# Value projection of the scans: four jobs of three token tiles by 256 channels become three jobs of two tiles by 512

## Chip, core and metric

One core of one Trainium2 chip. The time is the device time of one execution, in microseconds (us). The core's engines run their own instruction queues in order and meet on semaphores: TensorE (PE, matmuls; its weight loads are PEld), VectorE (DVE), ScalarE (ACT), GpSimd (POOL), and SyncE (SP), which issues the loads from HBM.

## The reference, cut to what matters

Two layers of a hybrid token mixer over 512 latent and 256 context tokens (768 rows here, D = 1024), all in fp32. Each layer projects the normed tokens `h` by one wide matrix and cuts the columns among three branches:

```
z = h @ w_in                       # (768, 1024) @ (1024, D_IN)
(aq, ak, av, gq, gk, gv, gr, ga, rq, rk, rv, rg, mg) = split_in(z)
o_a = window_attention(qa, ka, va, ...)              # 8 heads of 64, 2 key heads
o_g = bidir_scan(gq, gk, gv, decays from ga)         # gated linear attention, 4 heads, dv 128
o_r = bidir_scan(rq, rk, rv, fixed decays)           # retention, 4 heads, dv 128
y = sum(sigmoid(mg_z) * (o_z @ w_branch_z)) @ w_out  # merge, then a gated MLP with a convolution
```

The change concerns the two value projections `gv` and `rv` of each layer: 768 tokens by 1024 rows by 512 channels, four times in the program (two scans, two layers). Their results are wanted with tokens on the partitions.

## The kernel before

The program is one list of jobs, walked by `flow` (L486). An ordinary job (`chunk`, L457) makes 128 output channels for all tokens: the weight block is stationary, the tokens `h` stream by in pieces of 512 and 256 columns. Precision is kept by splitting weights and tokens into a high and a low part: three passes per 128-row block k, high by high, high by low, low by high. Tokens come split in `hh` and `hl`. Weights are split job by job in `split_w` (L431): a raw tile of 128x512 is loaded by SP (`load`, L421), ACT copies it to the high part (L452), and DVE or POOL subtracts (L454) to give the low one. All three tiles come from one ring of 12 buffers (`wp`, L319).

A value job (`Wide`, L208, `chunk_wide` L474) turns the roles round: a 128-token tile of `h` is stationary and the weights stream by, so that the result has tokens on the partitions. `value_jobs` (L915) makes four jobs per scan: two halves of 256 channels, each by tiles 0 to 2 and 3 to 5. A raw tile holds two row blocks of 256 channels, so a half takes four loads and four splits; the second job of a half shares the first one's (`share`). The gated linear attention's splits are subtracted on POOL (`job.pool`), the retention's on DVE. In `flow` (L531 to L547) a value job with its own weights finds the first two splits made during the job before and puts the other two into the queues after its first row block; a shared one puts those of the next job there. `prev.evac` (after the first row block of the next job) moves the finished PSUM tile to SBUF on ACT.

Beside the jobs runs side work, written as generators that put a step into the queues at every `yield`: `att_mix` (L816, window attention) beside the jobs of gated linear attention, `gla_mix` (L981) beside those of retention. Each pass of a job calls `beat` (L374), which adds the pass's matmul budget times a rate (`RATE`, L188: 2.0 and 1.65 steps per us beside gated linear attention, 0.693 and 0.655 beside retention, in layers 0 and 1) and issues a step for each whole unit. The budget of a scan's value jobs is 31.1 us (`cost`, L216), before and after the change; that of an ordinary job is 7.8 us (5.2 with 512 tokens). So the order on every engine is the program's order: a split stands behind each side step issued before it. `gla_mix` is hooked to the second value job of the retention (`J[1].pre`, L1357); it has 36 steps in layer 0 and 30 in layer 1, and is drained at the first gate job (`beside`, L1331). Its first phase runs three functions staggered over the six tiles: `logits` (one matmul L998, ACT L1000 to L1002, DVE L1003, ACT L1005, POOL L1006), `decays` (L1008) and `states` (L1084).

Of the kernel before, what the change touches and what calls it, by code (L numbers as in the profile page):

```python
# [11 lines left out]
AF = mybir.ActivationFunctionType  # L12
# [5 lines left out]
L, D, KD = 2, 1024, 8  # L18
TL, TC = 512, 256
TA = TL + TC  # L20
# [64 lines left out]
def pack(a):  # L85

    A = {k: np.asarray(v) for k, v in a.items()}
    f = np.float32

    def kp(m):  # L90
        return m.reshape(-1, 128, m.shape[-1]).transpose(1, 0, 2)

    def units(w):
        K, N = w.shape
        return w.reshape(K // 128, 128, N // 128, 128).transpose(2, 1, 0, 3)

    def wide(w):
        K, N = w.shape
        return w.reshape(K // 128, 128, N // 256, 256).transpose(2, 1, 0, 3)

    def rows(v, n=128):
        return np.broadcast_to(v, (n,) + v.shape).reshape(n, -1)

    r = {}
    r["x0"] = kp(np.concatenate([A["x"][0].T, A["ctx"][0].T], 1))
    con, ret = constants()
    r["con"], r["rcon"] = con, ret
    s = {}
    s["cc"] = kp(np.stack([A["c"][0], A["c_ctx"]], 1)).reshape(128, 16)
    s["adab"] = A["ada_b"].reshape(2, 48, 128).transpose(2, 0, 1).reshape(128, 96)  # L110
    s["n1g"] = A["norm1_g"].reshape(2, 8, 128).transpose(2, 0, 1).reshape(128, 16)
    s["n2g"] = A["norm2_g"].reshape(2, 8, 128).transpose(2, 0, 1).reshape(128, 16)
    s["qg"] = np.tile(A["attn_q_norm_g"].T, (2, 1))
    s["kg"] = np.tile(A["attn_k_norm_g"].T, (2, 1))
    s["sink"] = rows(A["attn_sink"])
    s["gng"] = A["gla_out_norm_g"].T
    s["rng"] = A["ret_out_norm_g"].T
    rd = A["ret_log_decay"]
    s["reta"] = rows(rd)
    pr = rd.reshape(2, 2, 2, 2)  # L120
    s["retb"] = np.concatenate([rows(pr[..., 0], 64), rows(pr[..., 1], 64)], 0)
    s["retc"] = np.concatenate([rows(rd[:, 0], 64), rows(rd[:, 1], 64)], 0)
    s["cw"] = A["ffn_conv_w"].reshape(2, 3, 44, 128).transpose(3, 0, 2, 1).reshape(128, 264)
    s["cb"] = A["ffn_conv_b"].reshape(2, 44, 128).transpose(2, 0, 1).reshape(128, 88)
    r["sml"] = np.concatenate([s[k] for k in SML], 1)

    r["ada"] = A["ada_w"][0][:, :2048].reshape(2, 4, 128, 2, 8, 128)[:, :, :, ::-1].transpose(4, 0, 2, 1, 3, 5)
    adt = A["ada_w"].transpose(0, 2, 1).reshape(2, 48, 128, 2, 512)
    r["adv"] = adt.transpose(0, 3, 1, 2, 4)
    r["crow"] = rows(np.stack([A["c"][0], A["c_ctx"]]).reshape(2, 2, 512).transpose(1, 0, 2))  # L130
    wi = A["w_in"]
    v0 = 512 + 128 + 128 + 256 + 256
    g0 = v0 + 512 + 512
    v1 = g0 + 32 + 256 + 256
    main = np.concatenate([wi[:, :, :v0], wi[:, :, v0 + 512:g0], wi[:, :, g0 + 32:v1], wi[:, :, v1 + 512:]], 2)
    r["wv"] = np.stack([np.stack([wide(wi[l, :, v:v + 512]) for v in (v0, v1)]) for l in range(L)])
    r["win"] = np.stack([units(main[l]) for l in range(L)])
    r["wga"] = np.stack([kp(wi[l, :, g0:g0 + 32]) for l in range(L)])
    gw = np.zeros((2, 98, 512), f)
    for n in (0, 32, 64):  # L140
        gw[:, n:n + 16, 0:256] = A["gla_gate_w"][:, 0]
        gw[:, n + 16:n + 32, 256:512] = A["gla_gate_w"][:, 1]
    gw[:, 96:98] = A["gla_gate_b"].reshape(2, 1, 512)
    r["gw"] = gw
    wb = A["w_branch"].copy()

    wb[:, 0] = wb[:, 0].reshape(2, 2, 4, 64, D).transpose(0, 2, 1, 3, 4).reshape(2, 512, D)
    r["wbr"] = np.stack([np.stack([units(wb[l, z]) for z in range(3)]) for l in range(L)])
    r["wo"] = np.stack([units(A["w_out"][l]) for l in range(L)])
    r["up"] = np.stack([units(A["ffn_up"][l]) for l in range(L)])  # L150
    r["dn"] = np.stack([units(A["ffn_down"][l]) for l in range(L)])
    return {k: np.ascontiguousarray(v.reshape(shape(k))) for k, v in r.items()}
# [1 line left out]

SHAPES = {
    "x0": (128, KD * TA), "con": (128, NCON), "rcon": (128, 512), "sml": (128, NSML),
    "ada": (16, 128, 1024), "adv": (L, 2, 48, 128, 512), "crow": (128, 2048), "win": (L, 46, 128, 1024), "wv": (L, 2, 2, 128, 2048), "wga": (L, 128, 256), "gw": (L, 98, 512),
    "wbr": (L, 3, 8, 128, 512), "wo": (L, 8, 128, 1024), "up": (L, 44, 128, 1024),
    "dn": (L, 8, 128, NFF * 128),
}  # L160
# [33 lines left out]
class Job:  # L194


    def __init__(self, src, h, cols, evac, nk=8, m=128, pre=None, share=None, late=False):
        self.src, self.h, self.cols, self.evac = src, h, cols, evac
        self.nk, self.m, self.pre, self.share, self.late = nk, m, pre, share, late
        self.ps = None  # L200
        self.raw, self.w, self.home, self.eager = [], [], None, ()
        self.pool = self.early = False
        self.wide, self.kp = False, 4

        self.both = m <= 64


class Wide(Job):  # L208


    def __init__(self, src, h, t0, evac, share=None):
        Job.__init__(self, src, h, [(0, TA)], evac, m=256, share=share)
        self.t0, self.wide, self.kp = t0, True, 2


def cost(cols):  # L216
# [96 lines left out]
class Prog:  # L313
# [117 lines left out]
    def split_w(self, job, part=1):  # L431

        if job is None:
            return
        if job.share:
            job.w = job.share.w
            return
        nc = self.nc
        self.load(job)
        for raw, n in job.raw[len(job.w):part + 1]:  # L440
            by_k = lambda v: v[:, 0:n].rearrange("p (k c) -> p k c", c=job.m)
            if job.home:
                k = job.kp * len(job.w)
                hi, lo = (v[:, k:k + n // job.m] for v in job.home())
            elif job.both:
                m = job.m
                both = self.wp.tile([128, 512], F32R, name="wb", tag="w")[:, 0:2 * n].rearrange("p (k c) -> p k c", c=2 * m)
                hi, lo = both[:, :, 0:m], both[:, :, m:2 * m]
            else:
                hi, lo = (by_k(self.wp.tile([128, 512], F32R, name=f"w{p}", tag="w")) for p in "hl")  # L450
            raw = by_k(raw)
            nc.scalar.activation(out=hi, in_=raw, func=AF.Copy)  # L452
            eng = nc.gpsimd if job.pool else nc.vector
            eng.tensor_tensor(out=lo, in0=raw, in1=hi.bitcast(F32), op=ALU.subtract)  # L454
            job.w.append((hi, both) if job.both else (hi, lo))

# [17 lines left out]
    def chunk_wide(self, job, k):  # L474

        nc = self.nc
        if job.ps is None:
            job.ps = self.pg()
        for n, (a, b) in enumerate(((0, 0), (1, 0), (0, 1))):
            for t in range(3):  # L480
                o = 128 * (job.t0 + t)
                nc.tensor.matmul(job.ps[:, 256 * t:256 * t + 256], job.h(k, b)[:, o:o + 128], job.w[k // 2][a][:, k % 2, :],  # L482
                                 start=(k == 0 and n == 0 and t != 1), stop=(k == job.nk - 1 and n == 2 and t > 0))
            self.beat(cost(job.cols) / 3)

    def flow(self, jobs):  # L486
# [5 lines left out]
        for item in jobs:  # L492
# [36 lines left out]
            self.split_w(job)  # L529
            n1, n2 = nxt(job, 1), nxt(job, 2)  # L530
            if job.wide:  # L531
                n3 = nxt(job, 3)
                for k in range(job.nk):
                    self.chunk_wide(job, k)
                    if k == 0:
                        prev.evac(prev.ps)
                    if not job.share:
                        if k == 0:
                            self.split_w(job, 3)
                        if k == 2:  # L540
                            self.load(n2, 4)
                            if not n2.wide:
                                self.load(n3)
                    elif k % 2 and (n1.wide or k == 3):
                        self.split_w(n1, k // 2)
                prev = job
                continue  # L547
            for k in range(job.nk):
# [366 lines left out]
    def value_jobs(self, l, scan, v):  # L915

        nc = self.nc

        jobs = []
        for j in range(2):  # L920
            for t in (0, 3):
                def evac(ps, j=j, t=t):
                    nc.scalar.activation(out=v()[:, t:t + 3, 256 * j:256 * j + 256],
                                         in_=ps[:, 0:TA].rearrange("p (t c) -> p t c", c=256), func=AF.Copy)

                jobs.append(Wide(self.i["wv"][l, scan, j], self.h, t, evac, jobs[-1] if t else None))
        return jobs


    def gla_jobs(self, l, nq):  # L930
# [775 lines left out]
```

## Time and profile before

| | |
|---|---|
| median of 3 runs | 2346.07 us (2345.8 to 2353.48) |
| profiled execution | 2355.63 us, span 2353.8 us |
| granted TensorE clock | 0.998 of full speed |
| PE busy | 2305.4 us, 98% |
| DVE / ACT / POOL busy | 60% / 40% / 13% |
| value matmuls (L482) | 1152 of 128x256, in four stretches from 151.5 to 1623.9 us |

In the profile's lines, L482 is the matmul of the value jobs, L470 that of the ordinary ones; `pg` is a job's PSUM tile, `wh` and `wl` are the weights' high and low parts, `raw` the loaded tile. "x3" counts merged instructions, an arrow reads "output from inputs", and brackets hold the idle time before an instruction with what ended it. PE's matmuls overlap, so the distance between starts, not the duration, is what one costs.

### The profile page before, as it was taken

Reading aid. Unit: us, or ns where it says so; the run is one execution under the profiler, and the core shown is the slowest. Engines: PE = TensorE matmul, PEld = TensorE weight load, DVE = VectorE, ACT = ScalarE, POOL = GpSimd, SP = SyncE. Lnnn points to the kernel's source line nnn. Section 1 sums busy time; section 2 is a strip of 40 time slices with the busy share of each in tenths; the row PEclk is TensorE's granted clock in tenths of the full one; section 3 lists DMA queues with packets and bytes.
Section 4 is the critical chain, followed back from the end, with each engine's and each line's share of the span. In section 5 each row is a group of like instructions: output and inputs, shape, how many; then the busy total and the mean of one; then the engine's idle time right before and its main releaser. Section 6 shows DMA issues by size and latency. Waiting matters only on the chain.

```text
span 2353.8 us, 35262 instructions
## 1 busy us (share of the span) xinstructions
PE 2305.4 (98%) x13570; PEld 1982.2 (84%) x13570; DVE 1415.1 (60%) x2870; ACT 930.5 (40%) x1622; POOL 298.8 (13%) x256
## 2 busy tenths in 40 slices
PE   7999999999999999999999999999999999999999
PEld 4888888888888888888888887989888888888887
DVE  5665475523777578766686656546753555645564
ACT  4665633322323253313313347555443335434342
POOL 0111164000111020000000014113500111000000
PEclk9999999999999999999999999999999999999999
DMA  7111112322454333353253331111333333232333
GB/s 257 54 39 46 44 59 90 95 65 79 139 161 157 104 95 118 120 186 97 88 188 99 96 106 65 50 46 38 101 114 112 95 103 113 97 96 98 99 99 99
DMA packets 132840, 235.79 MB, mean 100 GB/s; under 512 B 14460, under 2 KB 25980, under 8 KB 132544
## 3 DMA queue, kind: packets, MB, share of 16 engines
q1 hardware_dynamic: 123200, 223.57, 29.6%
q10 hardware_dynamic: 9472, 9.96, 1.2%
q8 instruction: 107, 1.75, 0.3%
q14 instruction: 61, 0.50, 0.1%
HBM read 220.37 MB, written 13.11 MB: 99 GB/s over the span
## 4 chain that ended last, share of the span: by engine, by line
PE 87%; DVE 5%; ACT 3%; issue 2%; POOL 1%; DMA 1%; SPq 0%; POOLq 0%; ACTq 0%; DVEq 0%
PE pg L470 73%; PE pg L482 5%; PE pm L908 2%; PE pm L897 1%; PE pm L1089 1%; PE ps L845 1%; PE ps L844 1%; PE pm L1111 1%; DVE qs L1052 1%; PE pm L1112 1%; DVE P L890 0%; PE pm L1275 0%; PE pm L613 0%; DVE Sg L1102 0%; DMA og<-o 0%
## 5 line engine op out<-in xcount | busy, mean ns | idle before, releaser
L470 PE MATMUL pg<-hh,wh 128*128 128x512 f32 (+1 forms) x2384 | 726.1, 357 | 6.6 <-DVE X L1317 1.5
L470 PE MATMUL pg<-hh,wl 128*128 128x512 f32 (+1 forms) x2384 | 722.2, 355 | 0.3 <-POOL wl L454 0.3
L470 PE MATMUL pg<-hl,wh 128*128 128x512 f32 (+1 forms) x2384 | 720.4, 354 | 0.9 <-POOL hl L305 0.7
L454 DVE TENSOR_TENSOR wl<-raw,wh 128x512 fp32r<-128x512 f32 x500 | 356.9, 722 | 335.8 <-ACT wh L452 284.0
L470 PEld LDWEIGHTS pg<-hh,wh 128*128 128x128 f32 x2384 | 397.5, 189 | 74.7 <-issue 4.5
L452 ACT ACTIVATE wh<-raw 128x512 fp32r<-128x512 f32 (+1 forms) x556 | 334.2, 619 | 309.6 <-PE pg L470 123.1
L470 PEld LDWEIGHTS pg<-hl,wh 128*128 128x128 f32 x2384 | 397.2, 189 | 66.3 <-POOL hl L305 1.4
L470 PEld LDWEIGHTS pg<-hh,wl 128*128 128x128 f32 x2384 | 395.4, 189 | 62.7 <-issue 1.3
L652 DVE SCALAR_TENSOR_TENSOR junk<-adr,crow 128x512 f32<-128x512 f32 x256 | 193.6, 756 | 9.1 <-DMA adr<-adv 2.9
L454 POOL TENSOR_TENSOR wl<-raw,wh 128x512 fp32r<-128x512 f32 x56 | 75.7, 1366 | 763.5 <-PE pg L470 556.4
L470 PE MATMUL pg<-al,wh 128*128 128x512 f32 (+1 forms) x500 | 154.2, 356 | 1.4 <-DVE al L572 1.4
L470 PE MATMUL pg<-ah,wh 128*128 128x512 f32 (+1 forms) x500 | 155.0, 358 | 0.0
L470 PE MATMUL pg<-ah,wl 128*128 128x512 f32 (+1 forms) x500 | 154.7, 357 | 0.0
L1306 POOL TENSOR_TENSOR M<-M,sg 128x768 f32<-128x768 f32 (+1 forms) x30 | 58.3, 1942 | 538.2 <-DVE sg L1304 538.2
L1294 ACT ACTIVATE sg<-pg 128x768 f32<-128x768 f32 (+1 forms) x48 | 33.7, 702 | 215.4 <-PE pg L470 215.4
L1479 DVE SCALAR_TENSOR_TENSOR acc<-pg,sml,acc 128x511 f32<-128x511 f32 (+1 forms) x129 | 84.8, 658 | 38.5 <-ACT acc L1476 38.3
L1317 DVE SCALAR_TENSOR_TENSOR X<-pg,mod,X 128x512 f32<-128x512 f32 (+1 forms) x72 | 45.7, 659 | 90.7 <-PE pg L470 90.7
L1476 ACT ACTIVATE acc<-pg,sml 128x768 f32<-128x768 f32 (+1 forms) x86 | 75.5, 878 | 59.6 <-PE pg L470 59.5
L470 PEld LDWEIGHTS pg<-al,wh 128*128 128x128 f32 x500 | 83.7, 188 | 16.9 <-DVE al L572 2.3
L470 PEld LDWEIGHTS pg<-ah,wh 128*128 128x128 f32 x500 | 83.9, 188 | 14.7 <-ACT ah L571 0.4
L470 PEld LDWEIGHTS pg<-ah,wl 128*128 128x128 f32 x500 | 83.4, 188 | 13.9
L1481 DVE SCALAR_TENSOR_TENSOR acc<-pg,sml,acc 128x511 f32<-128x511 f32 (+1 forms) x129 | 85.3, 661 | 4.6
(280 smaller groups left out, 3027.6 us busy)
## 6 DMA issues: line engine op xcount, KB each, us to landing
raw<-win SPq DMA_DIRECT2D x184, 256.0 KB, 2.9
raw<-up SPq DMA_DIRECT2D x176, 256.0 KB, 2.9
adr<-adv SPq DMA_DIRECT2D x160, 256.0 KB, 3.1
raw<-dn SPq DMA_DIRECT2D x64, 256.0 KB, 2.9
raw<-wbr SPq DMA_DIRECT2D x48, 256.0 KB, 2.7
aw<-ada SPq DMA_DIRECT2D x32, 256.0 KB, 5.4
raw<-wv SPq DMA_DIRECT2D x32, 256.0 KB, 3.1
raw<-wo SPq DMA_DIRECT2D x32, 256.0 KB, 3.0
```

The source lines that it names most:

```text
L452: nc.scalar.activation(out=hi, in_=raw, func=AF.Copy)
L454: eng.tensor_tensor(out=lo, in0=raw, in1=hi.bitcast(F32), op=ALU.subtract)
L470: nc.tensor.matmul(job.ps[0:m, lo:hi], job.w[k // 4][a][:, k % 4, :], job.h(k, b)[:, lo:hi], start=(k == 0 and n == 0), stop=(k == job.nk ...
L482: nc.tensor.matmul(job.ps[:, 256 * t:256 * t + 256], job.h(k, b)[:, o:o + 128], job.w[k // 2][a][:, k % 2, :], start=(k == 0 and n == 0 an ...
L652: nc.vector.scalar_tensor_tensor(out=junk, in0=raw, scalar=1.0, in1=cr[v], op0=ALU.mult, op1=ALU.mult, accum_out=acc)
L908: nc.tensor.matmul(po[64 * kv:64 * kv + 64, 0:256], self.att["Va"][:, kb, 64 * kv:64 * kv + 64], PT[b][:, 256 * kv:256 * kv + 256], start= ...
L1294: nc.scalar.activation(out=sgs[d][:, 0:n], in_=ps[:, 0:n], func=AF.Tanh, scale=0.5)
L1306: eng.tensor_tensor(out=m, in0=m, in1=sg[:, 0:n], op=ALU.add)
L1317: nc.vector.scalar_tensor_tensor(out=X(d)[:, lo:hi], in0=ps[:, lo:hi], scalar=gate(d, int(lo >= TL)), in1=xin[:, lo:hi], op0=ALU.mult, op1 ...
L1476: nc.scalar.activation(out=acc[:, 0:nq], in_=ps[:, 0:nq], func=AF.Identity, scale=cw(1), bias=self.s("cb", 44 * l + u))
L1479: nc.vector.scalar_tensor_tensor(out=acc[:, lo + 1:hi], in0=ps[:, lo:hi - 1], scalar=cw(0), in1=acc[:, lo + 1:hi], op0=ALU.mult, op1=ALU.add)
L1481: nc.vector.scalar_tensor_tensor(out=acc[:, lo:hi - 1], in0=ps[:, lo + 1:hi], scalar=cw(2), in1=acc[:, lo:hi - 1], op0=ALU.mult, op1=ALU.add)
```

## The change

Each scan's values become three jobs of two token tiles by all 512 channels, with 512-column matmuls. A job no longer shares weights: each of the three loads all eight row blocks (128x512, one per raw tile) and splits them. The loads go out five row blocks ahead, the splits two, spread over the job; from the last blocks on they are those of the next job. The subtract alternates between DVE and POOL. A job fills a PSUM tile of 1024 columns, evacuated in one piece, and the weights are packed to match.

```diff
--- before.py
+++ after.py
@@ -94,10 +94,6 @@
         K, N = w.shape
         return w.reshape(K // 128, 128, N // 128, 128).transpose(2, 1, 0, 3)
 
-    def wide(w):
-        K, N = w.shape
-        return w.reshape(K // 128, 128, N // 256, 256).transpose(2, 1, 0, 3)
-
     def rows(v, n=128):
         return np.broadcast_to(v, (n,) + v.shape).reshape(n, -1)
 
@@ -133,7 +129,7 @@
     g0 = v0 + 512 + 512
     v1 = g0 + 32 + 256 + 256
     main = np.concatenate([wi[:, :, :v0], wi[:, :, v0 + 512:g0], wi[:, :, g0 + 32:v1], wi[:, :, v1 + 512:]], 2)
-    r["wv"] = np.stack([np.stack([wide(wi[l, :, v:v + 512]) for v in (v0, v1)]) for l in range(L)])
+    r["wv"] = np.stack([np.stack([kp(wi[l, :, v:v + 512]) for v in (v0, v1)]) for l in range(L)])
     r["win"] = np.stack([units(main[l]) for l in range(L)])
     r["wga"] = np.stack([kp(wi[l, :, g0:g0 + 32]) for l in range(L)])
     gw = np.zeros((2, 98, 512), f)
@@ -154,7 +150,7 @@
 
 SHAPES = {
     "x0": (128, KD * TA), "con": (128, NCON), "rcon": (128, 512), "sml": (128, NSML),
-    "ada": (16, 128, 1024), "adv": (L, 2, 48, 128, 512), "crow": (128, 2048), "win": (L, 46, 128, 1024), "wv": (L, 2, 2, 128, 2048), "wga": (L, 128, 256), "gw": (L, 98, 512),
+    "ada": (16, 128, 1024), "adv": (L, 2, 48, 128, 512), "crow": (128, 2048), "win": (L, 46, 128, 1024), "wv": (L, 2, 128, 4096), "wga": (L, 128, 256), "gw": (L, 98, 512),
     "wbr": (L, 3, 8, 128, 512), "wo": (L, 8, 128, 1024), "up": (L, 44, 128, 1024),
     "dn": (L, 8, 128, NFF * 128),
 }
@@ -208,9 +204,9 @@
 class Wide(Job):
 
 
-    def __init__(self, src, h, t0, evac, share=None):
-        Job.__init__(self, src, h, [(0, TA)], evac, m=256, share=share)
-        self.t0, self.wide, self.kp = t0, True, 2
+    def __init__(self, src, h, t0, evac):
+        Job.__init__(self, src, h, [(0, 1024)], evac, m=512)
+        self.t0, self.wide, self.kp = t0, True, 1
 
 
 def cost(cols):
@@ -450,7 +446,7 @@
                 hi, lo = (by_k(self.wp.tile([128, 512], F32R, name=f"w{p}", tag="w")) for p in "hl")
             raw = by_k(raw)
             nc.scalar.activation(out=hi, in_=raw, func=AF.Copy)
-            eng = nc.gpsimd if job.pool else nc.vector
+            eng = nc.gpsimd if (len(job.w) % 2 if job.wide else job.pool) else nc.vector
             eng.tensor_tensor(out=lo, in0=raw, in1=hi.bitcast(F32), op=ALU.subtract)
             job.w.append((hi, both) if job.both else (hi, lo))
 
@@ -476,11 +472,12 @@
         nc = self.nc
         if job.ps is None:
             job.ps = self.pg()
-        for n, (a, b) in enumerate(((0, 0), (1, 0), (0, 1))):
-            for t in range(3):
+        hi, lo = job.w[k]
+        for n, (w, b) in enumerate(((hi, 0), (lo, 0), (hi, 1))):
+            for t in range(2):
                 o = 128 * (job.t0 + t)
-                nc.tensor.matmul(job.ps[:, 256 * t:256 * t + 256], job.h(k, b)[:, o:o + 128], job.w[k // 2][a][:, k % 2, :],
-                                 start=(k == 0 and n == 0 and t != 1), stop=(k == job.nk - 1 and n == 2 and t > 0))
+                nc.tensor.matmul(job.ps[:, 512 * t:512 * t + 512], job.h(k, b)[:, o:o + 128], w[:, 0, :],
+                                 start=(k == 0 and n == 0), stop=(k == job.nk - 1 and n == 2))
             self.beat(cost(job.cols) / 3)
 
     def flow(self, jobs):
@@ -529,20 +526,21 @@
             self.split_w(job)
             n1, n2 = nxt(job, 1), nxt(job, 2)
             if job.wide:
-                n3 = nxt(job, 3)
+
                 for k in range(job.nk):
                     self.chunk_wide(job, k)
                     if k == 0:
                         prev.evac(prev.ps)
-                    if not job.share:
-                        if k == 0:
-                            self.split_w(job, 3)
-                        if k == 2:
-                            self.load(n2, 4)
-                            if not n2.wide:
-                                self.load(n3)
-                    elif k % 2 and (n1.wide or k == 3):
-                        self.split_w(n1, k // 2)
+                    if k < 4:
+                        self.load(job, k + 5)
+                    elif n1.wide:
+                        self.load(n1, k - 3)
+                    elif k % 2 == 0:
+                        self.load(n1 if k == 4 else n2)
+                    if k < 6:
+                        self.split_w(job, k + 2)
+                    else:
+                        self.split_w(n1, k - 6)
                 prev = job
                 continue
             for k in range(job.nk):
@@ -916,15 +914,10 @@
 
         nc = self.nc
 
-        jobs = []
-        for j in range(2):
-            for t in (0, 3):
-                def evac(ps, j=j, t=t):
-                    nc.scalar.activation(out=v()[:, t:t + 3, 256 * j:256 * j + 256],
-                                         in_=ps[:, 0:TA].rearrange("p (t c) -> p t c", c=256), func=AF.Copy)
-
-                jobs.append(Wide(self.i["wv"][l, scan, j], self.h, t, evac, jobs[-1] if t else None))
-        return jobs
+        def evac(t):
+            return lambda ps: nc.scalar.activation(out=v()[:, t:t + 2, :], in_=ps.rearrange("p (t c) -> p t c", c=512), func=AF.Copy)
+
+        return [Wide(self.i["wv"][l, scan], self.h, t, evac(t)) for t in (0, 2, 4)]
 
 
     def gla_jobs(self, l, nq):
```

## Rows read from the trace of the kernel before

**Rows 1.** Page, part 4: shares of the span in the chain of waits, by line.

```profile
PE pg L470 73%; PE pg L482 5%; PE pm L908 2%; PE pm L897 1%; PE pm L1089 1%; PE ps L845 1%; PE ps L844 1%; PE pm L1111 1%; DVE qs L1052 1%; PE pm L1112 1%; DVE P L890 0%; PE pm L1275 0%; PE pm L613 0%; DVE Sg L1102 0%; DMA og<-o 0%
```

**Rows 2.** Windows of the four value stretches: busy us (instructions) by engine, clock, DMA share, GB/s.

```profile
151.54:210.96 59.42, 57.33 (x466) 53.34 (x465) 33.05 (x97) 32.77 (x72) 10.73 (x8) 1.00 0.16 51
244.97:300.71 55.74, 54.41 (x501) 50.77 (x499) 23.36 (x52) 32.98 (x64) 8.76 (x8) 1.00 0.16 53
1494.90:1552.20 57.30, 57.30 (x476) 53.88 (x476) 28.42 (x78) 30.26 (x62) 10.25 (x8) 1.00 0.16 53
1576.14:1623.90 47.76, 47.01 (x438) 45.62 (x437) 17.53 (x33) 27.89 (x51) 7.76 (x6) 1.00 0.17 55
```

**Rows 3.** Timeline of PE, second stretch of retention: start, us, engine, line, operation.

```profile
1580.92 0.52 PE L482 MATMUL pg<-wl,hh 128*128 128x256 f32 x3
1581.28 0.52 PE L482 MATMUL pg<-wh,hl 128*128 128x256 f32 x3
```

**Rows 4.** Timeline of PE in ordinary jobs of 512 columns.

```profile
2001.01 0.39 PE L470 MATMUL pg<-hh,wl 128*128 128x512 f32 x1
...
2005.78 0.39 PE L470 MATMUL pg<-hh,wl 128*128 128x512 f32 x1
```

**Rows 5.** Page, part 5: the weight splits (busy us, mean ns, idle before).

```profile
L454 DVE TENSOR_TENSOR wl<-raw,wh 128x512 fp32r<-128x512 f32 x500 | 356.9, 722 | 335.8 <-ACT wh L452 284.0
...
L452 ACT ACTIVATE wh<-raw 128x512 fp32r<-128x512 f32 (+1 forms) x556 | 334.2, 619 | 309.6 <-PE pg L470 123.1
...
L454 POOL TENSOR_TENSOR wl<-raw,wh 128x512 fp32r<-128x512 f32 x56 | 75.7, 1366 | 763.5 <-PE pg L470 556.4
```

**Rows 6.** Page, part 6: loads of the value weights (KB each, us to landing).

```profile
raw<-wv SPq DMA_DIRECT2D x32, 256.0 KB, 3.1
```

**Rows 7.** Timeline of ACT, first stretch of retention.

```profile
266.60 0.61 ACT L452 ACTIVATE wh<-raw 128x512 fp32r<-128x512 f32 x1
...
278.11 0.63 ACT L1005 ACTIVATE lgp<-lg 128x512 fp32r<-128x512 f32 x1 [0.82 <-DVE lg L1003]
278.65 0.58 ACT L1023 ACTIVATE eL<-ps 128x512 f32<-128x512 f32 x1
```

**Rows 8.** Timeline of PE, first stretch of retention.

```profile
260.95 0.52 PE L482 MATMUL pg<-wh,hh 128*128 128x256 f32 x3
...
274.94 0.40 PE L998 MATMUL pm<-gw,ga 98*128 98x512 f32 x1
...
276.61 0.64 PE L1013 MATMUL ps<-lgp,ts 128*128 128x256 f32 x4
...
277.96 0.62 PE L482 MATMUL pg<-wh,hl 128*128 128x256 f32 x3
```

**Rows 9.** Timeline of POOL, first stretch of retention.

```profile
266.77 1.30 POOL L1006 TENSOR_TENSOR lgp<-lg,lgp 128x512 fp32r<-128x512 f32 x1 [2.58 <-ACT lgp L1005]
...
278.82 1.28 POOL L1006 TENSOR_TENSOR lgp<-lg,lgp 128x512 fp32r<-128x512 f32 x1 [5.91 <-ACT lgp L1005]
```

**Rows 10.** Timeline of DVE, first stretch of retention.

```profile
267.25 1.37 DVE L454 TENSOR_TENSOR wl<-raw,wh 128x512 fp32r<-128x512 f32 x1 [1.22 <-ACT wh L452]
```

**Rows 11.** Timelines of ACT and PE, first stretch of gated linear attention.

```profile
176.38 0.62 ACT L452 ACTIVATE wh<-raw 128x512 fp32r<-128x512 f32 x1
181.73 0.62 ACT L452 ACTIVATE wh<-raw 128x512 fp32r<-128x512 f32 x1
...
176.05 0.52 PE L482 MATMUL pg<-wh,hl 128*128 128x256 f32 x3
...
180.39 0.52 PE L482 MATMUL pg<-wh,hl 128*128 128x256 f32 x3
```

**Rows 12.** Timeline of PE: idle before an instruction, in brackets, and its releaser.

```profile
174.98 0.87 PE L897 MATMUL pm<-con,P 128*128 128x128 f32 x4 [1.00 <-DVE P L890]
...
264.24 0.50 PE L1013 MATMUL ps<-lgp,ts 128*128 128x256 f32 x2 [0.90 <-POOL lgp L1006]
```

## Prediction

> **What bounds the kernel now.** I read the chain of waits first: the matmul line of the ordinary jobs holds 73% of it and the matmul line of the value jobs 5% [rows 1], so the time is that of TensorE (PE) working through its own program in order. Then I cut the trace into the four stretches in which value jobs run (gated linear attention and retention, in layers 0 and 1). They last 59.4, 55.7, 57.3 and 47.8 us, 220.2 us in all, and PE is busy in 216.0 of them (57.33 + 54.41 + 57.30 + 47.01); ScalarE (ACT) is busy 123.9, VectorE (DVE) 102.4, GpSimd (POOL) 37.5 [rows 2]. So nothing but PE is near full there, and PE loses only 4 us to waits. Third, the timeline of PE inside a stretch: the reader is to see passes of three 128x256 matmuls at 0.36 us start to start, with the side work's matmuls between them [rows 3, 8]. Last, the timelines of ACT, DVE and POOL in the third quarter of a stretch, to see when a weight split really runs after it was put into the queue [rows 7, 9, 10].
>
> **The change, part by part.**
>
> *Matmuls.* Before, each of the four scans runs 4 jobs x 8 row blocks x 3 passes x 3 = 288 matmuls of 256 columns, 1152 in all; after, 3 x 8 x 3 x 2 = 144 of 512, 576 in all. A 256-column one costs 0.120 us (three in 0.36) [rows 3]. A 512-column one with its own stationary load, from the ordinary jobs, costs (2005.78 - 2001.01)/21 = 0.227 us [rows 4]. So 138.2 us becomes 130.8: a gain of 7.4 us. Bounds: 0, if a 512 cost as much as two 256s, and 15 us, if it cost its columns alone (512 at the granted 2.4 GHz, 0.213 us). I take 7.4, measured on the same kind of matmul. The page "TensorE: Matmul & The Clock Gate" of the Trainium skill (section "Back-to-back issue gap") gives columns over 2.4 GHz plus about 2.5 ns for an isolated matmul; by that the halved count would save 576 x 2.5 ns = 1.4 us. The trace differs: 0.120 is 13 ns over its columns, 0.227 is 14 ns, and the rows decide.
>
> *Splits and loads.* Before, 8 splits per scan (one load, ACT copies the high part, DVE or POOL subtracts); after, 24: 64 more in all. ACT gets 64 x 0.619 = 39.6 us [rows 5], to 163.5 us of about 213, 77%. By turns the subtract is on DVE and POOL: DVE goes from 16 to 48 (32 x 0.722 = 23 us, to 125), POOL from 16 to 48 (32 x 1.366 = 44 us, to 81) [rows 2, 5]. No engine is full, so capacity costs nothing; what it costs is decided by when each split is late. The 64 loads of 256 KB add 16.8 MB on SP's queue. A load lands in 3.1 us [rows 6], goes out with chunk k and is split after chunk k+3, three chunks of at least 6 x 0.227 = 1.36 us later: 4.1 us, so it is covered; each takes the buffer of the load four chunks older, freed by its split. Evacuation moves the same 3072 columns per scan on ACT, in three pieces for four. None of this costs PE anything by itself.
>
> *The new wait.* Before, a value job had all its splits one job ahead or at its start. After, the split for chunk k+2 is put into the queues after chunk k, and PE must have its high part when chunk k+2 starts and its low part one pass (0.455 us) later. Only chunk k+1 lies between: 1.36 us plus the side work in it. ACT and POOL work in order, so the split stands behind all side work put in during chunk k. While PE waits, the side work's matmuls queued behind wait too, and with them the ACT and DVE steps that read their PSUM; nothing else of the program runs meanwhile. In the stretches of gated linear attention (their side work is the window attention) ACT keeps up: the splits ran 0.0 us and 1.0 us after their chunk's end (176.38 against 176.05 + 0.36, 181.73 against 180.39 + 0.36) [rows 11].
>
> In the retention stretches the side work is the GLA mix, whose logits step puts four ACT operations in a row, with a DVE operation before the fourth. From its matmul at 274.94, the next ACT operation behind the block starts at 278.65, 3.71 us later [rows 7, 8]. What that does to a split is already to be seen: one put in when the chunk starting at 260.95 began ran at 266.60, 5.65 us late, behind two such blocks [rows 7, 8]. Before, no one needs it soon; after, PE does. For one logits block at time 0: high part ready at 3.71 + 0.65 (266.60 to the subtract's start at 267.25) = 4.36 us. The low part: POOL has the block's own subtract from 3.88 to 5.16 (278.82, 1.28 long), so a POOL split is done at 5.16 + 1.29 = 6.45; the DVE split at 267.25 took 1.37 beside POOL's at 266.77, so a DVE split is done at 4.36 + 1.37 = 5.73 [rows 7, 9, 10].
>
> When PE wants it depends on the pass of chunk k after which the block was issued. The block's matmul takes 0.23, each left pass 0.455, chunk k+1 1.36, and the next side step (decays) 1.35 (276.61 to 277.96 [rows 8]); this step comes 3 or 4 passes later and so falls before chunk k+2, except half the time after the last pass. Wanted: after the first pass 0.23 + 0.91 + 1.36 + 1.35 = 3.85; after the second 3.40; after the last 1.59 or 2.94, mean 2.27. PE waits 0.51, 0.96 or 2.09, mean 1.19. The low part is then wanted at 4.36 + 0.455 = 4.82: 0.91 more on DVE, 1.63 on POOL, mean 1.27. Together 2.45 us for a block (ends: 0.5, with the low part hidden, and 2.77 + 1.63 = 4.4). The pacing (0.693 and 0.655 steps per us of matmul budget, the blocks at steps 1, 2, 4, 7, 10 and 13 of the side work, 20.7 us of budget in the second and third job) puts six blocks per stretch into value jobs; I leave out the last of layer 1, whose split is already one for the next, ordinary job: 11 blocks x 2.45 = 27 us (ends 5.5 and 48). Stalls in PE of 2 us that these stretches have now, such as the 0.90 us on POOL's logits subtract at 264.24 [rows 12], go, since PE comes later: -2.
>
> In the two stretches of gated linear attention, a POOL split put in at a lag of 0 to 1.0 us is done 0.65 + 1.37 later (2.0 to 3.0), and wanted after 1.36 + side + 0.455, about 2.7 with the mean side work (22 us per 24 chunks, what is left of 57 after 288 x 0.12). So perhaps a third of 12 wait 0.5 us, and the transposes that already wait 1.00 us for DVE [rows 12] wait 0.7 more in one case or two: 3 us per stretch, 6 in all (ends 0, and 24 splits x 0.3 per stretch, 14).
>
> *The side work's start.* The GLA mix is hooked to the second value job, which now begins after a third instead of a quarter of the scan: 2.6 us of budget less. At the two rates 51.8 and 46.6 us give 35.9 and 30.5 steps for 36 and 30, with the first one early at the older, faster rate. I take 0; if the last step spills into the drain, 2 us.
>
> *Sum.* -7.4 + 27 - 2 + 6 = +23.6 us. The profiled execution took 2355.63 us (span 2353.8 and 1.8 around it), 9.6 above the median of the runs, 2346.07; all terms are differences, so I add them to the median: 2369.7, say 2370.
>
> **The rivals.**
> *Covered.* ACT runs so far ahead that the splits are ready, and only the matmul gain is left: 2346 - 7 = 2339, with small stalls up to 2350. For it: before, no value matmul waits for a split, and 56% busy ACT has room. Against: the 5.65 us. It decides if splits behind a logits block come less than about 3 us after it.
> *The port lock.* POOL's subtracts hold up DVE's, and not only behind logits blocks: the DVE split at 267.25 took 1.37 where the mean is 0.722 [rows 5, 10]. If each of the other 37 POOL splits costs PE the 0.65 us by which DVE was held up, 37 x 0.65 = 24 us come on top: 2394. Against: POOL already runs eight operations in each gated linear attention stretch, splits among them, with PE busy 96 and 100% of it [rows 2]. By the page "SBUF — State Buffer" of the Trainium skill (section "Who interferes with whom") a DVE instruction with two SBUF inputs and a GpSimd one that reads SBUF exclude each other for the whole instruction; the trace agrees (267.25 + 1.37 = POOL's end at 268.07 plus 0.55).
> *Late loads.* SP's in-order queue or buffers freed late make each chunk wait for its weights: if PE waits 0.5 us in half of the 96 chunks, +24 without the logits stalls less the gain, 2363. Against: 3.1 against 4.1 us.
>
> **How the numbers follow.** Forecast 0.68 (own range 2353 to 2392), covered 0.15, port lock 0.12, late loads 0.05. Range 2352 to 2393: it leaves out most of "covered" and half of the lock. About 0.5% (11.7 us) is what a measurement of this kernel can tell from no change: slower 0.78, same 0.18 (most of "covered" and the low end of the forecast), faster 0.04, since the whole matmul gain is under 0.5%.
>
> **What would show it.** Right: about 576 matmuls on the value line at 0.227 us spacing; PE idle in the two retention stretches of some 13 us each, released by the ACT and POOL/DVE lines of the split, each soon after a logits matmul; the other two stretches within 2 us of their old length. Wrong: PE busy through the retention stretches; or idle released by DMA (late loads); or idle spread evenly over all POOL splits (the lock).

## The result, and the profile after

The kernel after takes 2397.03 us (2393.48 to 2403.94, six runs) where the kernel before took 2346.01 in the same comparison: a ratio of 1.022 [1.0203, 1.0237], 51 us slower. The prediction had the sign and the first mechanism right, but not the size: 24 us were expected, and 51 lies above the range. Two things that its sum put at nothing make most of the difference (see why the prediction was wrong).

The page after: the granted clock in 40 slices, the shares of the chain, the splits' ACT half and the loads (against [rows 1], [rows 5] and [rows 6]).

```profile
PEclk9999899999999999999999999999999999999999
...
PE pg L466 69%; PE pg L479 2%; PE pm L1082 1%; PE pm L906 1%; PE pm L895 1%; PE pm L1104 1%; PE pm L1105 1%; ACT wh L448 0%; DVE qs L1045 0%; POOL ks L1045 0%; PE pm L1268 0%; POOL wl L450 0%; PE ps L842 0%; POOL hl L301 0%; PE ps L1214 0%
...
L448 ACT ACTIVATE wh<-raw 128x512 fp32r<-128x512 f32 x620 | 373.6, 619 | 310.0 <-PE pg L466 116.9
...
raw<-wv SPq DMA_DIRECT2D x96, 256.0 KB, 2.7
```

In the lines of after, L466 is the ordinary matmul, L479 the value matmul, L448 and L450 the two halves of a split, L991 to L999 the logits block, L1059 the scores of the GLA mix with L1066 on DVE behind them. The splits are the 64 more that were counted (620 for 556), at the duration taken (619 ns). They now stand in the chain of waits, as does POOL's half, each with under half a percent; no load does, though there are 96 for 32. The clock digits show an 8 in the slice of the first retention stretch. Windows of the four value stretches (first to last value matmul) and of the jobs behind each retention stretch, until the last output of the GLA mix: columns as in [rows 2].

```profile
148.06:208.24 60.18, 57.15 (x317) 43.44 (x316) 39.43 (x108) 39.31 (x85) 15.47 (x12) 1.00 0.33 111
241.70:310.96 69.26, 58.47 (x318) 43.82 (x317) 27.44 (x50) 39.75 (x75) 23.14 (x19) 0.90 0.27 92
310.96:382.80 71.84, 65.61 (x472) 58.03 (x471) 49.53 (x86) 22.53 (x40) 39.69 (x39) 0.93 0.16 56
1511.74:1572.41 60.67, 59.41 (x350) 45.93 (x348) 35.55 (x91) 38.33 (x79) 15.84 (x12) 1.00 0.33 111
1594.04:1656.72 62.68, 52.23 (x285) 41.48 (x284) 19.84 (x33) 34.39 (x61) 22.52 (x18) 0.89 0.30 103
1656.72:1713.10 56.38, 50.32 (x340) 43.15 (x339) 39.68 (x73) 19.48 (x36) 30.16 (x28) 0.94 0.16 53
```

The same windows of before, cut in the same way (those of [rows 2] run on for up to 0.9 us, and its third stops 2.1 us short of the last value matmul).

```profile
151.54:210.25 58.71, 56.62 (x461) 52.63 (x460) 32.75 (x97) 32.47 (x71) 10.73 (x8) 1.00 0.16 51
244.97:299.78 54.81, 53.48 (x493) 49.84 (x490) 23.27 (x52) 32.98 (x64) 8.76 (x8) 1.00 0.17 54
299.78:358.80 59.02, 56.59 (x426) 50.02 (x425) 46.71 (x81) 20.91 (x36) 40.74 (x39) 1.00 0.17 58
1494.94:1554.30 59.36, 59.36 (x494) 55.27 (x493) 28.72 (x80) 31.03 (x65) 10.25 (x8) 1.00 0.16 52
1576.14:1623.84 47.70, 46.95 (x438) 45.56 (x437) 17.47 (x33) 27.89 (x51) 7.76 (x6) 1.00 0.17 55
1623.84:1668.30 44.46, 42.67 (x322) 37.47 (x321) 36.32 (x64) 14.82 (x28) 26.79 (x26) 1.00 0.16 54
```

Three things are to be seen. The retention stretches grew by 14.5 and 15.0 us, the gated linear attention ones by 1.5 and 1.3. Of the 29.4 us, 19.2 are PE idle (10.79 + 10.45 against 1.33 + 0.75) and 10.3 are PE busy longer with fewer matmuls, at a mean clock of 0.90 and 0.89. And the ordinary jobs behind grew too, by 12.8 and 11.9 us, with their clock at 0.93 and 0.94, though no line of theirs was changed.

PE's waits in the two retention stretches of after, and in the window behind the first: us, times, longest.

```profile
PE pg L479 <- ACT wh L448: 5.2, 6, 2.3
PE pg L479 <- POOL wl L450: 2.9, 3, 1.3
PE pg L479 <- DVE wl L450: 1.4, 2, 0.7
...
PE pg L479 <- ACT wh L448: 7.2, 4, 2.6
PE pg L479 <- POOL wl L450: 3.2, 4, 1.4
...
PE ps L1059 <- DVE ab L1066: 5.2, 3, 2.7
```

Value matmuls wait 19.9 us for splits and none for a DMA. One such wait, on PE and on ACT (first retention stretch):

```profile
260.18 0.39 PE L991 MATMUL pm<-gw,ga 98*128 98x512 f32 x1
...
261.77 0.39 PE L991 MATMUL pm<-gw,ga 98*128 98x512 f32 x1
262.00 0.62 PE L479 MATMUL pg<-wl,hh 128*128 128x512 f32 x2
262.46 0.61 PE L479 MATMUL pg<-wh,hl 128*128 128x512 f32 x2
265.40 0.87 PE L479 MATMUL pg<-wh,hh 128*128 128x512 f32 x2 [2.33 <-ACT wh L448]
...
270.53 1.05 PE L479 MATMUL pg<-wh,hh 128*128 128x512 f32 x2
271.38 1.05 PE L479 MATMUL pg<-wl,hh 128*128 128x512 f32 x2
```

```profile
260.61 0.60 ACT L993 ACTIVATE ab<-pm 128x512 f32<-128x512 f32 x1 [1.42 <-PE pm L991]
...
263.29 0.63 ACT L998 ACTIVATE lgp<-lg 128x512 fp32r<-128x512 f32 x1 [0.76 <-DVE lg L996]
263.83 1.01 ACT L918 ACTIVATE rv<-pg 128x1024 f32<-128x1024 f32 x1
264.73 0.62 ACT L448 ACTIVATE wh<-raw 128x512 fp32r<-128x512 f32 x1
```

The split stands behind the four ACT steps of the logits block and the evacuation, and PE waits 2.33 us for it. Before the wait a pass of two matmuls takes 0.46 us (262.00 to 262.46); after it, from 270.53 to 271.38, 0.85: PE has fallen from 2.4 to 1.2 GHz. The clock stands at 1.2 GHz for 14.4 and 13.7 us of the two stretches, in seven spells: six begin within 2.5 us of the end of a wait of 1.3 us or more for a split, the seventh behind two waits of 0.7 to 0.8 us. In before it stood at 2.4 through both.

### The profile page after: what moved, and what is told of

It is laid out like the page before. It is cut to its first block, busy times and chain, and to the rows that moved or that the text cites. A ratio compares the mean times of both kernels' runs of the same rounds, so it can differ in the third digit from the quotient of the medians.

```text
span 2400.4 us, 34468 instructions
## 1 busy us (share of the span) xinstructions
PE 2321.8 (97%) x12994; PEld 1963.7 (82%) x12994; DVE 1437.6 (60%) x2902; ACT 964.7 (40%) x1682; POOL 340.7 (14%) x288
## 4 chain that ended last, share of the span: by engine, by line
PE 76%; DVE 3%; ACT 2%; issue 2%; POOL 1%; DMA 0%; POOLq 0%; ACTq 0%; DVEq 0%
PE pg L466 69%; PE pg L479 2%; PE pm L1082 1%; PE pm L906 1%; PE pm L895 1%; PE pm L1104 1%; PE pm L1105 1%; ACT wh L448 0%; DVE qs L1045 0%; POOL ks L1045 0%; PE pm L1268 0%; POOL wl L450 0%; PE ps L842 0%; POOL hl L301 0%; PE ps L1214 0%
## 5 line engine op out<-in xcount | busy, mean ns | idle before, releaser
L466 PE MATMUL pg<-hh,wh 128*128 128x512 f32 (+1 forms) x2384 | 725.2, 356 | 8.1 <-ACT hh L1647 2.1
L466 PE MATMUL pg<-hl,wh 128*128 128x512 f32 (+1 forms) x2384 | 721.8, 355 | 0.9 <-POOL hl L301 0.7
L466 PE MATMUL pg<-hh,wl 128*128 128x512 f32 (+1 forms) x2384 | 721.1, 355 | 0.7 <-DVE wl L450 0.4
L450 DVE TENSOR_TENSOR wl<-raw,wh 128x512 fp32r<-128x512 f32 (+1 forms) x532 | 381.5, 724 | 369.8 <-ACT wh L448 314.4
L448 ACT ACTIVATE wh<-raw 128x512 fp32r<-128x512 f32 x620 | 373.6, 619 | 310.0 <-PE pg L466 116.9
L466 PEld LDWEIGHTS pg<-hh,wh 128*128 128x128 f32 x2384 | 397.3, 190 | 74.1 <-issue 4.4
L466 PEld LDWEIGHTS pg<-hl,wh 128*128 128x128 f32 x2384 | 398.4, 190 | 64.5 <-POOL hl L301 1.4
L466 PEld LDWEIGHTS pg<-hh,wl 128*128 128x128 f32 x2384 | 396.6, 189 | 63.8 <-issue 1.5
L450 POOL TENSOR_TENSOR wl<-raw,wh 128x512 fp32r<-128x512 f32 x88 | 118.9, 1358 | 820.4 <-PE pg L466 550.6
L466 PE MATMUL pg<-al,wh 128*128 128x512 f32 (+1 forms) x500 | 154.8, 358 | 1.5 <-DVE al L570 1.5
L466 PE MATMUL pg<-ah,wh 128*128 128x512 f32 (+1 forms) x500 | 153.9, 356 | 0.0
L466 PE MATMUL pg<-ah,wl 128*128 128x512 f32 (+1 forms) x500 | 153.6, 355 | 0.0
L466 PEld LDWEIGHTS pg<-al,wh 128*128 128x128 f32 x500 | 83.7, 188 | 15.9 <-DVE al L570 2.4
L466 PEld LDWEIGHTS pg<-ah,wl 128*128 128x128 f32 x500 | 83.9, 188 | 14.3
L466 PEld LDWEIGHTS pg<-ah,wh 128*128 128x128 f32 x500 | 83.4, 188 | 14.3 <-ACT ah L569 0.4
```

The lines of the kernel that those rows point to most:

```text
L466: nc.tensor.matmul(job.ps[0:m, lo:hi], job.w[k // 4][a][:, k % 4, :], job.h(k, b)[:, lo:hi], start=(k == 0 and n == 0), stop=(k == job.nk ...
```

## The experiments

The expectations name three theories: J, that the just-in-time split behind the logits block is the loss; L, that the GLA mix, hooked to the second value job and so started a third of a scan in instead of a quarter, runs late into the ordinary jobs; and C, that what is left is a collision in the jobs behind, of DVE's state updates with POOL's work. Each kernel is told by its difference to before in five parts of its profiled execution, in us: both gated linear attention stretches (G), the retention stretches (R0, R1), each from the first to the last start of a value matmul, and what follows each retention stretch (T0, T1), until the first of the transposes that close the gated linear attention (L1268 in after, L1275 in before), so that the side work of the retention lies in T too. Idle and "1.2 GHz" are the time in R and T, all four together, in which no matmul ran or the granted clock stood at its lower level; before has 8.8 and 0. The last column is the ratio of the timed runs. The five parts of after come to 56 where the medians differ by 51: the profiled execution of before is 9.6 us above its median, mostly outside these parts, and that of after 5 above its own. Each row of the table is one execution, so a few us between two rows can be chance. Of the edits below only the lines that matter are shown.

| kernel | G | R0 | T0 | R1 | T1 | idle | 1.2 GHz | ratio |
|---|---|---|---|---|---|---|---|---|
| after | 2.8 | 14.5 | 10.3 | 15.0 | 13.6 | 37.0 | 51.2 | 1.022 [1.0203, 1.0237] |
| e1_hook | 2.7 | 17.1 | 5.8 | 14.2 | 3.8 | 34.1 | 34.1 | 1.0176 [1.0159, 1.0193] |
| e2_ahead3 | 7.3 | -0.3 | 6.4 | 0.5 | 13.7 | 21.5 | 17.1 | 1.0098 [1.0083, 1.0113] |
| e3_before_late | 0.0 | 0.1 | 4.1 | -0.2 | 11.6 | 15.6 | 20.5 | 1.0048 [1.0033, 1.0063] |
| e4_no_splits | -3.4 | 0.2 | 7.7 | 2.8 | 13.7 | 21.3 | 30.7 | 1.0062 [1.0044, 1.008] |
| e5_dve | 4.6 | 9.2 | 8.0 | 11.7 | 12.4 | 33.9 | 30.7 | 1.0213 [1.0199, 1.0227] |
| e6_hook_ahead3 | 6.9 | 5.5 | 5.8 | 1.4 | 2.2 | 18.2 | 17.1 | 1.0085 [1.0071, 1.0099] |
| e7_by_scan | 5.8 | 3.6 | 5.4 | 1.4 | 3.8 | 18.5 | 17.1 | 1.0089 [1.0075, 1.0103] |
| e8_hook_no_splits | -3.4 | 10.3 | 4.5 | 4.1 | 2.2 | 23.2 | 23.9 | 1.0071 [1.0055, 1.0086] |
| e9_hook7 | 5.7 | 2.8 | 3.8 | 1.2 | 3.1 | 16.5 | 10.2 | 1.0061 [1.0044, 1.0079] |
| e10_ks_dve | 8.8 | 4.3 | 3.3 | 1.9 | 2.2 | 15.5 | 13.7 | 1.0074 [1.0059, 1.0089] |

**Splits three row blocks ahead**, in after:

```diff
-                    if k < 6: self.split_w(job, k + 2)
-                    else: self.split_w(n1, k - 6)
+                    if k < 5: self.split_w(job, k + 3)
+                    elif n1.wide or k > 5: self.split_w(n1, k - 5 if n1.wide else k - 6)
```

(the loads six ahead instead of five).

> The changed kernel with splits three row blocks ahead instead of two (loads as before five to six ahead). Theory J (splits just in time behind logits blocks stall PE, and the stalls bring half clock): PE's waits on the split lines fall from 57 us (both PE queues added) to under 15, the retention stretches shrink from 69.7 and 62.8 to about 58 and 51 us, total 2370 to 2378. Rival P (subtracts on POOL and DVE hold each other up, an engine's capacity): 2388 or more, waits on POOL and DVE subtracts unchanged.

Measured: 2371.2 us, 26 below after. Windows of its two retention stretches:

```profile
244.32:298.86 54.54, 51.00 (x318) 39.31 (x317) 25.42 (x49) 39.19 (x75) 22.97 (x19) 1.00 0.37 121
...
1580.11:1628.30 48.19, 45.29 (x285) 36.99 (x284) 20.75 (x33) 34.10 (x61) 22.80 (x18) 1.00 0.42 134
```

Same instructions, same busy ACT and POOL, yet the stretches are back at 54.5 and 48.2 us, PE busy falls to 51.0 and 45.3, and the clock is 1.00. So both parts of their 29 us, the waits and the slower clock, hang on the one block of lead. T0 and T1 stay at +6.4 and +13.7: that is another cause. G grew by 4.5 more.

**The mix started early**, in after, and **late**, in before:

```diff
# e1_hook: at block 6 of the first value job, a quarter of the scan
-        J[1].pre = lambda: self.side.append(paced(self.gla_mix(l, nq), RATE[l][2]))
+        J[0].at = (6, lambda: self.side.append(paced(self.gla_mix(l, nq), RATE[l][2])))
# e3_before_late: before's second job, at block 3, about a third of the scan
+        J[1].at = (3, lambda: self.side.append(paced(self.gla_mix(l, nq), RATE[l][2])))
```

(`flow` calls `at[1]()` when it comes to row block `at[0]` of the job; those lines are left out here.)

> The changed kernel with one edit: the GLA mix is hooked in at block 6 of the first value job of the retention, the same point of the matmul budget (a quarter of the scan) as before the change. Theory L (late start: the 22 us that the ordinary jobs behind the two retention stretches have gained, +10.5 and +11.9, come from the mix starting a third of the way in): 2375 to 2385 us, those jobs back within 5 us of before. Rival T (they come from the stalls and the half clock left by the value jobs): 2392 to 2400 us.

> The kernel before with one edit: the GLA mix is hooked in at block 3 of the second value job of the retention (11 of 32 blocks, a third of the scan), no new splits. Theory L: 2356 to 2368 us, the time lost in the ordinary jobs behind the value jobs. Rival T: 2346 to 2350.

Measured: e1 2389.31 us, 8 below after, T1 from 13.6 to 3.8, the retention stretches unmended: between the two expectations. Its T0 of 5.8 holds one wait of 6.82 us that after does not have; it is taken up with e6. e3 took 2359.64 us against 2349.33 for before measured beside it: 10 us lost (11 by the ratio) with no split and no matmul changed, nearly all in T0 and T1, as theory L has it. How, in e3's PE behind the second retention stretch (L1069 are the scores, L471 the ordinary matmul):

```profile
1663.41 2.08 PE L1069 MATMUL ps<-qs,ks 64*128 64x128 f32 x16 [3.00 <-DVE ab L1076]
...
1667.29 0.63 PE L471 MATMUL pg<-hl,wh 128*128 128x512 f32 x1
1667.71 0.63 PE L471 MATMUL pg<-hh,wl 128*128 128x512 f32 x1
```

```profile
1655.94 3.17 DVE L1055 TENSOR_TENSOR qs<-gqk,ec 64x256 f32<-64x256 f32 x4
1659.14 1.11 DVE L455 TENSOR_TENSOR wl<-raw,wh 128x512 fp32r<-128x512 f32 x1
...
1660.78 0.71 DVE L666 STREAM_SHUFFLE sw<-rqk 128x512 f32<-128x512 f32 x1
...
1662.59 0.67 DVE L1076 SCALAR_TENSOR_TENSOR ab<-ps,con 128x512 f32<-128x512 f32 x1
```

The scores of the next tile wait for their PSUM until DVE has read the last ones. On DVE that step (`at`, `ab`) stands behind a split of an ordinary job and the retention's rotation. PE waits 3.00 us, and then a matmul starts every 0.42 us: 1.2 GHz again. After has the same wait four times, 6.9 us in all and up to 2.7 long; before, with the mix earlier, has it twice, 1.5 us in all and up to 0.8 long.

**No splits inside a job**, in after: six of each value job's eight row blocks use the two splits already there, so 72 of the 96 loads and splits of the values are left out, and the values are wrong.

```diff
-        hi, lo = job.w[k]
+        hi, lo = job.w[k % 2]
```

> The changed kernel without six of the eight loads and splits of each value job: every block multiplies one of the job's first two weight tiles, so the values are wrong; matmuls, order and hook stay. It prices the matmuls and the late hook alone, with no split to wait for. Matmul gain 7 us and theory L: 2349 to 2362 us. Matmul gain and rival T: 2337 to 2343.

Measured: 2362.59 us, 34 below after and just above the expected span; T0 and T1 stay at 7.7 and 13.7 (10.3 and 13.6 in after). G is 3.4 us *below* before: here the gain of the wider matmuls is seen, 1.2 us in the layer 1 stretch, in which neither kernel has an idle PE (59.36 to 58.12).

**All value subtracts on DVE**, in after:

```diff
-            eng = nc.gpsimd if (len(job.w) % 2 if job.wide else job.pool) else nc.vector
+            eng = nc.gpsimd if job.pool and not job.wide else nc.vector
```

> The changed kernel with every subtract of the value jobs on DVE instead of every second on POOL. Theory J (a split is late because ACT runs it behind the logits block; the subtract adds to it): the high parts stay late, the low parts come some 0.7 us sooner for half of the splits; POOL waits of 22.6 us go, DVE waits rise from 4.9 to 10 or 15, waits on ACT stay near 30; 2385 to 2398 us. Rival P (POOL's subtracts and the shared port are the cause): 2375 or less.

Measured: 2395.2 us, not told apart from after. What ended the idle time of PE's two queues (matmuls and weight loads) before value matmuls, after and e5:

```profile
  ACT wh L448: 29.7, 24
  POOL wl L450: 22.6, 26
  DVE wl L450: 4.9, 8
```

```profile
  ACT wh L448: 31.8, 27
  DVE wl L450: 16.5, 26
```

With POOL out of it the wait only changes its name: it is the ACT half that is late, and the subtract follows it. That sets the rival of the port lock, as it was priced, aside.

**Both mendings**: e1's edit and e2's.

> Both mendings: splits three row blocks ahead, GLA mix hooked in at block 6 of the first value job. If the just-in-time splits and the late start are all that costs, the matmul gain of 7 us is left, less the 3 or 4 us per stretch that the gated linear attention stretches lost to DVE in the run with splits three ahead: 2342 to 2350 us. If something else in the change costs (capacity, port, loads): 2352 or more.

Measured: 2365.98 us, a miss by 16 to 24 us. T1 is mended; G (+6.9), R0 and T0 are not. In R0 PE waits 0.9 us twice for the two parts of one tile's logits (263.89 and 265.31) and then runs 6.8 us at 1.2 GHz. In T0 stands one long wait, here in e6's PE, DVE and POOL, followed by the same steps of before on DVE and POOL:

```profile
320.44 2.95 PE L1062 MATMUL ps<-qs,ks 64*128 64x128 f32 x16 [6.83 <-DVE qs L1048]
```

```profile
310.48 9.37 DVE L1098 SCALAR_TENSOR_TENSOR Sg<-Sg,E 64x128 f32<-64x128 f32 x16
319.88 2.20 DVE L1048 TENSOR_TENSOR qs<-gqk,ec 64x256 f32<-64x256 f32 x5
```

```profile
310.79 6.44 POOL L1048 TENSOR_TENSOR ks<-gqk,en 64x256 f32<-64x256 f32 x8 [10.89 <-ACT en L1042]
```

```profile
304.28 4.39 DVE L1102 SCALAR_TENSOR_TENSOR Sg<-Sg,E 64x128 f32<-64x128 f32 x16
```

```profile
307.07 3.07 POOL L1052 TENSOR_TENSOR ks<-gqk,en 64x256 f32<-64x256 f32 x2 [12.47 <-DVE Sg L1102]
```

The 16 state updates take 4.39 us in before and 9.37 in e6, where nine of them have a step of POOL beside them, mostly `ks`, and need some 0.8 us each (311.01 to 318.43); `qs`, which PE needs, is late by it. In before POOL began its `ks` at 307.07, when more than half of the updates were done, and the updates did not slow down: there POOL's two `ks` took 3.07 us, where e6's eight took 6.44. The same wait, 6.82 or 6.83 us long, stands in e1, e7 and e8, all hooked at block 6, and not in after.

**What is left, three ways.** e7 is e6 with the subtracts of gated linear attention all on POOL, those of retention all on DVE; e9 is e6 with the hook one block later, at 7; e10 is e6 with `ks` of the first two tiles on DVE.

```diff
# e7_by_scan: the engine of the subtract
+            eng = nc.gpsimd if job.pool else nc.vector
# e9_hook7
+        J[0].at = (7, lambda: self.side.append(paced(self.gla_mix(l, nq), RATE[l][2])))
# e10_ks_dve: the engine of ks
+            nc.vector if t in order[:2] else nc.gpsimd
```

> As the run before it, with the subtracts of the gated linear attention's value jobs all on POOL and those of the retention's all on DVE, as before the change. The waits of the transposes on DVE in the gated linear attention stretches (1.97, 1.15, 1.60, 1.16 us with splits three ahead) should shrink by half: 2338 to 2346 us, 3 to 5 below the run before it. If POOL's 24 subtracts of 1.3 us come too late for PE there, no gain or a loss of a few us.

> Splits three ahead with the GLA mix hooked in at block 7 of the first value job instead of 6 (1.3 us of budget later). Theory C (in layer 0 the wait of 6.83 us behind the retention stretch is an accident of order: DVE's sixteen state updates meet POOL's key products and take 9.37 instead of 4.39 us): another point moves the meeting, the wait changes by 3 us or more, total 2356 to 2362 us. If it is a settled cost of the extra splits: wait and total as with block 6, within 3 us.

> Splits three ahead, hook at block 6, and the key products of the GLA mix's first two tiles on DVE instead of POOL, so that POOL reads nothing while DVE updates the states. Theory C: the sixteen updates go back from 9.37 to 4.4 us, PE's wait of 6.83 us falls to 4 or less though DVE has 3 us more to do, the half clock behind it goes, total 2356 to 2361 us. If the updates are slow for another reason: no change, 2364 to 2368.

Measured: e7 2365.57 us, no difference and a miss. e9 2362.45, just above the span that theory C gave: the lowest median of the new form, though its interval overlaps that of e6, and 15 us behind before. The wait of 6.83 is gone, and the largest of T0 in its place is 2.3. e10 2365.32, a miss in the time, though its 16 updates are back at 4.39 us (from 309.12), with nothing on POOL beside them, and the wait shrank to one of 3.5 and one of 1.1 us, now for `ks` on DVE, and T0 with it, from 5.8 to 3.3. G, which the edit does not touch, came out 1.9 longer in that execution, with 6.8 us at 1.2 GHz where e6 had 3.4.

So C is a true wait of a few us and not the rest of the loss. G is a rest common to e2, e6, e7, e9 and e10. PE's waits in all of e9, and in all of before:

```profile
PE pm L898 <- DVE P L891: 7.1, 6, 2.0
...
PE ps L845 <- DVE st L857: 4.5, 8, 1.2
```

```profile
PE pm L897 <- DVE P L890: 3.2, 3, 1.1
PE ps L844 <- DVE st L856: 2.9, 4, 1.2
```

PE waits longer for the window attention's steps on DVE, by 5.5 us in all; within the G stretches it is 7.1 us for 2.1, which is most of e9's 5.7. This rest comes with the splits: without 72 of them (e4, and e8 below) G is 3.4 us shorter than before. The subtracts on DVE are not its main part, since e7, which has none of the gated linear attention's there, still has 5.8. Which part of the splits it is, and why three blocks of lead make it worse than two (G 2.8 in after), was not isolated.

**Early mix, no splits inside a job**: e4's edit and e1's (72 splits left out again).

> The changed kernel with the GLA mix hooked in at block 6 of the first value job, and without six of the eight loads and splits of each value job (the blocks multiply the job's first two weight tiles again, so the values are wrong): the new matmuls with neither their splits nor the late start. If the splits and the start are all that the change costs: 2336 to 2344 us. If the 512-column matmuls give nothing, or something else in the order costs: 2348 or more, and the retention stretches are no shorter than before.

Measured: 2364.34 us, a miss: R0 is 10.3 us longer than before, though three quarters of the splits are gone. Its PE:

```profile
251.89 0.39 PE L988 MATMUL pm<-gw,ga 98*128 98x512 f32 x1
...
252.58 0.39 PE L988 MATMUL pm<-gw,ga 98*128 98x512 f32 x1
...
259.40 1.22 PE L480 MATMUL pg<-wh,hh 128*128 128x512 f32 x2 [5.07 <-ACT wh L449]
```

The splits that remain, those of the next job, go out in blocks 6 and 7, and the hook at block 6 puts two logits blocks 0.69 us apart in front of them: 5.07 us of wait, the longest of this kind in any run, from two splits. e1 has the same one (5.1). In the retention stretches the number of splits is not what costs (e2 makes all of them there in the old time); their place behind logits blocks is.

## Why the prediction was wrong, step by step

- *What bounds the kernel, and where*: right. PE alone was near full, and the loss lies in the retention stretches and behind them.
- *Matmuls, -7.4*: right in the distance (0.46 for two, [rows 4] gave 0.227 for one); the gain seen without waits was 1.2 us in a stretch against 1.85.
- *Splits and loads cost nothing by themselves*: right in the retention stretches. ACT, DVE and POOL have the counted work, and e2 does all of it there in the old time. No wait of PE is for a load. In the stretches of gated linear attention it is not shown: e2 is 7.3 us longer there, and e4 without most splits 3.4 shorter.
- *The new wait, 27 us less 2*: the mechanism is right, and e2 and e5 show it; the size came out as 19.9 us of waits, idle up by 19.2. The waits for the high part were sized well, 11 x 1.19 = 13.1 us forecast and 12.4 measured (5.2 + 7.2); those for the low part came out at half, 7.5 us for 11 x 1.27 = 14.0.
- *A term that was not there*: the clock. The sum counted a wait as idle time only. Behind the waits above PE ran at 1.2 GHz ([rows 2] show 1.00 throughout): 28 us of it in the two stretches, where PE was busy 10.3 us longer although its matmuls should have become cheaper by 3.7 (half of 28 less 3.7 is 10.3). So the retention stretches lost 29.4 us where the steps gave 27 - 2 - 3.7 = 21.3.
- *Gated linear attention, +6 less its matmul gain of 3.7*: the net of 2.3 is near the 2.8 us measured, but by luck. By the windows above PE's idle time grew by 2.2 us there and not by 6, and its busy time grew by 0.6 where 3.7 less was expected.
- *The step that failed*: "The side work's start ... I take 0; if the last step spills into the drain, 2 us." It compared budget with steps inside the value jobs and left out what the later steps meet in the jobs behind them: T0 and T1 lost 10.3 and 13.6 us, 24 in all. e3 shows it alone: 15.6 us in these five parts, 11 in the timed runs, from the later start only. With e2's lead, T0 + T1 still lose 20; with e1's hook 10, of which 6.8 are the one wait that this hook brought in. The lost time is again waits, up to 2.7 us long, and the spells at 1.2 GHz behind them.
- *The rivals*: "covered" and "late loads" are excluded by the waits, the port lock, as it was priced, by e5. DVE and POOL do hold each other up, but at the state updates (9.37 for 4.39 us), when the mix starts at another moment. The page "SBUF — State Buffer" of the Trainium skill (section "Who interferes with whom") says that a DVE instruction with two SBUF inputs contends with a GpSimd instruction that reads SBUF. The rows of e6 agree, where both inputs of a state update lie in SBUF; so does e10, which has nothing on POOL there and 4.39 us again.

By parts the loss of after is 2.8 + 29.4 + 23.9 = 56 us, of which 28 are more idle PE in R and T and, by an estimate, about 25 the lower clock (half of 51.2 us, if PE was busy in them). The two mendings take back 31 of the 51 us in e6 and 36 in e9. What remains open is the rest of the new form: 15 us in e9, spread as 5.7 in G, 4.0 in R and 6.9 in T; and how much of the 1.2 GHz time a given wait brings on, which differed from run to run (6.8 us in G of e10, 3.4 in G of e6, none in G of e9 with the same waits).

## What to carry to other kernels

A weight split that was made long ahead cost PE no wait here; the same split made two blocks ahead stands, in its engine's order, behind whatever side work was queued in between, so ask for each just-in-time step what the longest block in front of it is, and give it that much lead. When job boundaries move, everything hooked to them moves too: follow the moved work to where it ends, not only to where it begins. And in a kernel that PE bounds, price a wait of one to three microseconds at more than itself, since the matmuls behind it may run at half the clock, as here.

## What was not expected of the hardware

- With PE near full before and behind the wait, the granted clock fell to 1.2 GHz behind single waits of 2.3 to 3.0 us (after at 265.40, e3 at 1663.41), and value passes took 0.85 us for 0.46. In before none of R and T ran at that level, in after 51.2 us of it. Not every such wait did it: in e2 the clock stayed at 2.4 GHz through T0, with a wait of 2.76 us at 359.2.
- A DVE state update of 64x128 takes 0.27 us (16 in 4.39) and took some 0.8 with POOL at work beside it (nine in e6, 311.01 to 318.43). In before, where POOL's `ks` began late among the updates, it was POOL that took longer.
